# A softmax with relative-position bias: the last row of the fourth chunk's first load as two transfers, over 120 and over 8 partitions

## The chip, the cores and the metric

The kernel runs on one core of a Trainium2 chip. The metric is the device time of one execution in microseconds; where several runs are shown, their median counts. Of the core's engines the kernel uses the vector engine (DVE), the scalar engine (ACT), the synchronisation engine (SP), which only issues transfers, and for two tiny set-up instructions GpSimd (POOL). Transfers between the chip's memory (DRAM) and the on-chip memory (128 partitions) are carried by 16 DMA engines. SP and ACT each have a queue of their own on all 16.

## The reference

For two batches, eight heads and 2112 positions, `logits` holds 2 x 8 square matrices of 2112 x 2112 float32. To each element a bias is added that depends on its head and on the clipped distance of its row and column, and then a softmax goes along each row.

```
pos = np.arange(S)
rel = pos[:, None] - pos[None, :]
rel_clipped = np.clip(rel, -max_rel, max_rel) + max_rel      # max_rel = 16
bias = rel_bias[:, rel_clipped].copy()                        # (H, S, S)
logits = logits + bias[None, :, :, :]
logits = logits - logits.max(axis=-1, keepdims=True)
exp = np.exp(logits)
return (exp / exp.sum(axis=-1, keepdims=True)).astype(np.float32)
```

285 MB are read and 285 MB are written; the arithmetic per element is small.

## The kernel before, in words

**Tiling.** The 8 x 2112 rows of one batch are dealt to the 128 partitions in runs of RP = 132 neighbouring rows, so 16 partitions share a head. The kernel works through a partition's 132 rows in K = 11 rounds of G = 12 rows. A round has NBUF = 4 chunks: two of R = 6 rows of the first batch and the same two of the second. A chunk is thus 128 partitions x 6 rows x 2112 columns (on each partition 50,688 contiguous bytes in DRAM), and there are 44 chunks. Chunk m of every round lives in buffer X[m]; the four buffers are all there is. The order listings call the four buffers X_58 to X_61.

**Loads (SP).** Lines 97 and 98 issue the loads of the first round's four chunks at once, one after the other, without a wait. Then the loop of lines 99 to 102 goes over rounds and chunks: it waits until the store from X[m] has landed (semaphore st[m]) and issues the next load into X[m]. A load raises ld[m] by 16 when all of it has landed.

**The DVE's loop** (lines 222 to 226). At the start of a round `window` copies the bias row that this round needs (L172). For each chunk `add` waits for ld[m] and then goes through the six rows (L186): it adds the bias, negates, and takes the row's extremum into `nmax`. `scale` waits until the ACT has done the six exponentials, takes the reciprocals of the sums (L210) and multiplies four of the six rows (L213). Then comes the next chunk.

**The ACT's loop** (lines 227 to 231). `exps` takes each row as soon as the DVE has added to it and writes the exponentials and their sums (L197); `scale_rest` multiplies the last two rows (L218); `store` waits until all six rows are scaled and issues the chunk's store to `out` (L95).

**What sets the order.** Nothing but the code's order on each engine and the semaphores; there is no scheduler. L88 is the helper `take`, which waits for a semaphore and lowers it again. On every DMA engine the loads stand in SP's queue and the stores in ACT's, each in the order of issue.

**Around these** stand a set-up that builds the bias row on each partition from `rel_bias` (lines 119 to 169), for which the ACT issues one small load over 4 partitions (L122), and at the end SP's wait for the last four stores (lines 103 and 104).

The lines that the change touches are the four first loads (97, 98) and the wait at the head of `add` (183).

Of the kernel before, what the change touches and what calls it, by code (L numbers as in the profile page):

```python
# [15 lines left out]
def kernel(  # L16
# [6 lines left out]
    nc = tc.nc  # L23
    P = 128
    B, H, S, S2 = logits.shape
# [3 lines left out]
    RP = H * S // P  # L29
# [4 lines left out]
    NBUF = 4  # L34
    R = 6
    M = NBUF // B
    G = M * R
# [6 lines left out]
    X = [io.tile([P, R * S], FP32, tag=f"X{b}", name=f"X{b}") for b in range(NBUF)]  # L44
# [22 lines left out]
    def view(t, offset, dims):  # L67
        return bass.AP(tensor=t.tensor, offset=t.offset + offset, ap=[[list(t.ap[0])[0], P]] + dims)

    def rows(t, k, m):  # L70
        return bass.AP(
            tensor=t.tensor, offset=t.offset + (m // M) * (H * S * S) + (m % M) * R * S + k * (G * S), ap=[[RP * S, P], [1, R * S]],
        )

    with tc.tile_critical(no_gpsimd_drain=True):  # L75
        ld = [nc.alloc_semaphore(f"ld{b}") for b in range(NBUF)]
        st = [nc.alloc_semaphore(f"st{b}") for b in range(NBUF)]
# [2 lines left out]
        scaled = nc.alloc_semaphore("scaled")  # L80
        inv = nc.alloc_semaphore("inv")
        rb = nc.alloc_semaphore("rb")
        zero = nc.alloc_semaphore("zero")
        idx = nc.alloc_semaphore("idx")
        dve = nc.alloc_semaphore("dve")

        def take(eng, sem, n):
            eng.wait_ge(sem, n).then_inc(sem, -n)  # L88

        def load(k, m):  # L90
            nc.sync.dma_start(out=X[m][:, :], in_=rows(logits, k, m)).then_inc(ld[m], 16)

        def store(k, m):
            take(nc.scalar, scaled, R)
            nc.scalar.dma_start(out=rows(out, k, m), in_=X[m][:, :]).then_inc(st[m], 16)  # L95

        for m in range(NBUF):
            load(0, m)
        with nc.Fori(0, K - 1, 1, engines=[ENG.SP]) as k:
            for m in range(NBUF):  # L100
                take(nc.sync, st[m], 16)
                load(k + 1, m)
# [3 lines left out]
        v = nc.vector  # L106
# [6 lines left out]
        def settle():  # L113
# [9 lines left out]
            out=bass.AP(tensor=F2.tensor, offset=F2.offset, ap=[[Q * step, P // Q], [1, H * W]]),  # L123
            in_=bass.AP(tensor=rel_bias.tensor, offset=rel_bias.offset, ap=[[0, P // Q], [1, H * W]]),
# [15 lines left out]
        for o, n, s, op in ((eq, NB, q, ALU.is_equal), (lt, NB, q, ALU.is_lt), (hsel, H, h, ALU.is_equal),  # L140
# [24 lines left out]
                           in_=view(reg, 1, [[1, NB - 1], [0, RP - W]])))  # L165
# [9 lines left out]
        def row(m, i):  # L175
            return X[m][:, i * S : (i + 1) * S]

        def col(t, m, i, n=1):
            c = m * R + i
            return t[:, c : c + n]  # L180

        def add(m):
            take(v, ld[m], 16)
            for i in range(R):
                x = G - 1 - (m % M) * R - i
                v.tensor_tensor_reduce(  # L186
                    out=row(m, i), in0=row(m, i), in1=F2[:, x : x + S],
                    scale=-1.0, scalar=BIG, op0=ALU.add, op1=ALU.min, accum_out=col(nmax, m, i),
                ).then_inc(added, 1)
# [32 lines left out]
        with nc.Fori(0, K, 1, engines=[ENG.DVE]) as k:  # L222
            window(k)
            for m in range(NBUF):
                add(m)
                scale(m)
        with nc.Fori(0, K, 1, engines=[ENG.Activation]) as k:
            for m in range(NBUF):
                exps(m)
                scale_rest(m)  # L230
                store(k, m)
# [31 lines left out]
```

## Time and profile before

| | |
|---|---|
| three runs | 1325.74, 1325.94, 1336.57 us |
| median | 1325.94 us |
| the profiled execution, first to last instruction (span) | 1323.8 us |
| DVE busy | 866.2 us, 65% |
| ACT busy | 757.2 us, 57% |
| bytes moved by DMA | 570.98 MB, 431 GB/s over the span |
| each of 44 loads and 44 stores | 6336 KB |
| median from issue to landing | loads 38.4 us, stores 59.0 us |

The profile is of one execution. Its span leaves out what lies before the first instruction and after the last; it is 2.1 us, or 0.16%, below the median of the three runs. The busy times of the engines overlap each other. A landing is the moment when all 16 DMA engines have reported their share of a transfer. In the DMA views a queue's row holds its packets, the MB they carry, and the time they took as a share of 16 engines over the stretch; q1 is SP's queue, q10 ACT's. Timeline rows start with the start and the length in microseconds, then engine, line, operation and tiles; in square brackets is the idle time before the instruction, and what ended it.

### The profile page before, as it was taken

The numbers are of one execution on the slowest core, as the hardware profiler recorded it, in microseconds if no ns is written. First come the engines' busy times: TensorE is split into PE (matmuls) and PEld (weight loads), VectorE is DVE, ScalarE is ACT, GpSimd is POOL, SyncE is SP. The second block draws the span as 40 slices with busy tenths as digits, with TensorE's granted clock in tenths as the row PEclk, the third lists the DMA queues.
The fourth block names the chain that finished last, engine by engine and source line by source line (L and its number), as shares of the span: only waits on it lengthen the run. The fifth ranks groups of instructions, "written<-read, shape, count | busy, mean of one in ns | idle before, by whom it ended". The sixth has DMA issues, their size and how long they took to land. (4 is left out here: it accounts for less than half of the span.)

```text
span 1323.8 us, 2109 instructions
## 1 busy us (share of the span) xinstructions
DVE 866.2 (65%) x781; ACT 757.2 (57%) x627; POOL 0.4 (0%) x6
## 2 busy tenths in 40 slices
DVE  6886666566766675576667666556766576566662
ACT  3776655556666555555656555555666565555663
POOL 0000000000000000000000000000000000000000
DMA  9999999999999999999999999999999999999998
GB/s 417 417 423 435 441 435 423 441 438 421 440 441 427 430 441 435 424 440 438 424 437 440 437 423 440 440 421 438 441 432 426 441 437 423 440 440 423 437 441 369
DMA packets 12682, 570.98 MB, mean 431 GB/s; under 512 B 1412, under 2 KB 1416, under 8 KB 1416
## 3 DMA queue, kind: packets, MB, share of 16 engines
q1 hardware_dynamic: 6336, 285.48, 50.0%
q10 hardware_dynamic: 6344, 285.48, 49.8%
q14 instruction: 2, 0.02, 0.0%
HBM read 285.48 MB, written 285.47 MB: 431 GB/s over the span
## 5 line engine op out<-in xcount | busy, mean ns | idle before, releaser
L197 ACT ACTIVATE X<-X,nmax 128x2112 f32<-128x2112 f32 x264 | 542.6, 2055 | 505.1 <-DVE nmax L186 472.4
L186 DVE CUSTOM_DVE_ANT_0 X<-X,F 128x2112 f32<-128x2112 f32 x264 | 605.2, 2354 | 319.1 <-DVEq L88 319.1
L213 DVE TENSOR_SCALAR X<-X,rec 128x2112 f32<-128x2112 f32 x176 | 220.3, 1315 | 2.8
L218 ACT ACTIVATE X<-X,rec 128x2112 f32<-128x2112 f32 x88 | 176.1, 2048 | 17.2 <-DVE rec L210 12.2
L210 DVE RECIPROCAL rec<-tot 128x6 f32<-128x6 f32 x44 | 8.4, 191 | 106.2 <-DVEq L88 106.2
L197 ACT ACTIVATION_READ_ACCUMULATOR X<-X,nmax 128x1 f32 x264 | 49.2, 186 | 0.0
L197 ACT ACT_TABLE_LOAD x11 | 14.1, 1283 | 22.6 <-ACTq L88 19.9
L172 DVE COPY F<-F 128x2123 f32 x11 | 26.0, 2361 | 0.5 <-DVEq L88 0.5
L186 DVE DVE_READ_ACCUMULATOR2_ANT nmax<- 128x1 f32 x264 | 21.6, 82 | 0.0
L144 DVE LOAD_MASK_SELECT F<-F x1 | 0.0, 14 | 6.2 <-DMA F<-in_rel_bias_dram 6.2
L164 DVE COPY F<-own 128x1485 f32<-128x1485 f32 x1 | 1.7, 1698 | 0.0
L120 DVE MEMSET F<- 128x264 f32 x1 | 0.3, 278 | 1.1 <-SPq L75 1.1
L142 DVE TENSOR_SCALAR Z<-rec,Z 128x16 f32<-128x16 f32 (+2 forms) x5 | 0.8, 233 | 0.1
L163 DVE TENSOR_TENSOR F<-F,own 128x528 f32<-128x528 f32 x1 | 0.7, 717 | 0.1
L160 DVE TENSOR_TENSOR F<-Z,own 128x528 f32<-128x528 f32 x1 | 0.7, 705 | 0.0
L150 DVE TENSOR_REDUCE own<-F 128x33 f32<-128x264 f32 x1 | 0.6, 609 | 0.1
L147 DVE TENSOR_TENSOR F<-F,Z 128x264 f32<-128x264 f32 x1 | 0.4, 429 | 0.1
L144 DVE STREAM_SHUFFLE F<-F 128x264 f32<-128x264 f32 x1 | 0.4, 442 | 0.0
L158 DVE SCALAR_TENSOR_TENSOR own<-Z,own 128x16 f32<-128x16 f32 x1 | 0.2, 235 | 0.2 <-DVEq L88 0.2
L155 DVE TENSOR_SCALAR own<-Z,own 128x16 f32<-128x16 f32 x1 | 0.2, 235 | 0.2 <-DVEq L88 0.2
L166 DVE COPY F<-own 128x115 f32<-128x115 f32 x1 | 0.3, 271 | 0.0
L168 DVE COPY F<-own 128x115 f32<-128x115 f32 x1 | 0.3, 271 | 0.0
(11 smaller groups left out, 1.6 us busy)
## 6 DMA issues: line engine op xcount, KB each, us to landing
X<-in_logits_dram SPq DMA_DIRECT2D x44, 6336.0 KB, 38.4
out_dram<-X ACTq DMA_DIRECT2D x44, 6336.0 KB, 59.0
F<-in_rel_bias_dram ACTq DMA_DIRECT2D x1, 4.1 KB
```

The source lines that it names most:

```text
L142: then(v.tensor_scalar(out=o, in0=num[:, 0:n], scalar1=s, scalar2=None, op0=op))
L144: then(v.stream_shuffle(out=T, in_=T, mask=[0] * Q))
L150: then(v.tensor_reduce(out=rbK, in_=view(F2, H * W, [[1, W], [W, H]]), axis=mybir.AxisListType.X, op=ALU.add))
L160: then(v.tensor_tensor(out=bands, in0=view(eq, 0, [[1, NB], [0, W]]), in1=view(rbK, W - 1, [[0, NB], [-1, W]]), op=ALU.mult))
L163: then(v.tensor_tensor(out=bands, in0=bands, in1=view(rest, 0, [[1, NB], [0, W]]), op=ALU.add))
L164: then(v.tensor_copy(out=view(F, C0 + W, [[RP, NB - 1], [1, RP - W]]), in_=view(reg, 1, [[1, NB - 1], [0, RP - W]])))
L172: then(v.tensor_copy(out=F2[:, 0:SW], in_=F[:, bass.ds(RP - G - k * G, SW)]))
L186: v.tensor_tensor_reduce(out=row(m, i), in0=row(m, i), in1=F2[:, x : x + S], scale=-1.0, scalar=BIG, op0=ALU.add, op1=ALU.min, accum_out=c ...
L197: nc.scalar.activation(out=row(m, i), in_=row(m, i), func=ACTF.Exp, scale=-1.0, bias=col(nmax, m, i), accum_out=col(tot, m, i),).then_inc( ...
L210: v.reciprocal(out=col(rec, m, 0, R), in_=col(tot, m, 0, R)).then_inc(inv, 1 if m < NBUF - 1 else NBUF + 1)
L213: v.tensor_scalar_mul(out=row(m, i), in0=row(m, i), scalar1=col(rec, m, i)).then_inc(scaled, 1)
L218: nc.scalar.activation(out=row(m, i), in_=row(m, i), func=ACTF.Copy, scale=col(rec, m, i),).then_inc(scaled, 1)
```

## The change

The first load of the fourth chunk (m = 3, buffer X_61) is issued in three pieces: rows 0 to 4 of all 128 partitions, which still raise ld[3]; then row 5 of partitions 0 to 119; then row 5 of partitions 120 to 127. The last two raise a new semaphore, head3. The DVE's `add` waits, for this buffer, also until head3 is at least 32. That wait doesn't lower head3, so from the second round on it is met at once. All later loads, and the first loads of the other three chunks, are as before.

```
@@ part: a view of DRAM that takes rows a to b of n partitions from p on
+    def part(t, k, m, a, b, p=0, n=P):
+        return bass.AP(
+            tensor=t.tensor, offset=t.offset + (m // M) * (H * S * S) + ((m % M) * R + a) * S + k * (G * S) + p * RP * S,
+            ap=[[RP * S, n], [1, (b - a) * S]],
+        )
+
...
+        head3 = nc.alloc_semaphore("head3")
...
+        def load_part(eng, m, a, b, sem, p=0, n=P):
+            eng.dma_start(out=X[m][p : p + n, a * S : b * S], in_=part(logits, 0, m, a, b, p, n)).then_inc(sem, 16)
+
...
-        for m in range(NBUF):
+        for m in range(NBUF - 1):
             load(0, m)
+        UP = P - P // 16
+        load_part(nc.sync, NBUF - 1, 0, R - 1, ld[NBUF - 1])
+        load_part(nc.sync, NBUF - 1, R - 1, R, head3, 0, UP)
+        load_part(nc.sync, NBUF - 1, R - 1, R, head3, UP, P - UP)
...
         def add(m):
             take(v, ld[m], 16)
+            if m == NBUF - 1:
+                v.wait_ge(head3, 32)
             for i in range(R):
```

SP's instructions at the start of the program, before the change: the four first loads, and then the first rows of the loop (ISA is the wait for a store).

```order
L91 DMA X_58<-in_logits_dram 128x12672
L91 DMA X_59<-in_logits_dram 128x12672
L91 DMA X_60<-in_logits_dram 128x12672
L91 DMA X_61<-in_logits_dram 128x12672
L99 UNCONDITIONAL_BRANCH
L91 ISA
L91 DMA X_58<-in_logits_dram 128x12672
```

The same place of SP with the change (the numbers of the lines are those of the changed kernel):

```order
L98 DMA X_58<-in_logits_dram 128x12672
L98 DMA X_59<-in_logits_dram 128x12672
L98 DMA X_60<-in_logits_dram 128x12672
L101 DMA X_61<-in_logits_dram 128x10560
L101 DMA X_61<-in_logits_dram 120x2112
L101 DMA X_61<-in_logits_dram 8x2112
L113 UNCONDITIONAL_BRANCH
L98 ISA
L98 DMA X_58<-in_logits_dram 128x12672
```

One transfer of 12672 columns has become three, of 10560, 2112 and 2112 columns, in the same place ahead of the loop. On the DVE and the ACT no instruction is added or moved; only the first add of buffer X_61 waits for two semaphores in place of one.

## The prediction

> **What bounds the kernel now.** I read the page first: the busy shares, the DMA line and the queues.
>
> ```profile
> DVE 866.2 (65%) x781; ACT 757.2 (57%) x627; POOL 0.4 (0%) x6
> ...
> DMA  9999999999999999999999999999999999999998
> ...
> DMA packets 12682, 570.98 MB, mean 431 GB/s; under 512 B 1412, under 2 KB 1416, under 8 KB 1416
> ...
> q1 hardware_dynamic: 6336, 285.48, 50.0%
> q10 hardware_dynamic: 6344, 285.48, 49.8%
> ```
>
> No compute engine is above 65%, and the DMA engines are busy in every slice. q1 carries the loads (SP), q10 the stores (ACT). 6336 packets for 44 loads are 144 each: 128 data packets, one per partition (six rows, 50,688 B), and 16 small ones that raise the semaphore, one per DMA engine. So an engine gets 8 data packets and one count per transfer.
>
> Next the DMA view of one whole round of four chunks in the middle, 200 to 319.6 us:
>
> ```profile
> q1 hardware_dynamic: 576, 25.95, 50.1%
> q10 hardware_dynamic: 575, 25.90, 50.0%
> ```
>
> 51.85 MB over 16 engines and 50,688 B are 63.9 packets per engine in 119.6 us: **1.871 us per packet**. The whole kernel has 704 per engine, 1317 us of the 1323.8 us span, so at most 6 or 7 us can be gained anywhere. The waits agree: the DVE's largest wait is that of its add (L186) for a load, through the semaphore instruction of L88.
>
> ```profile
> DVE X L186 <- DVEq L88: 319.1, 42, 8.5
> ```
>
> What is left to decide is how the two queues stand to each other. I call **lead** the number of data packets by which an engine's load queue is ahead of its store queue. The DMA view from 0 to 85.3 us (about where the fourth load has landed), then from 85.3 to 115.1 us:
>
> ```profile
> q1 hardware_dynamic: 588, 26.56, 74.1%
> q10 hardware_dynamic: 204, 9.13, 24.7%
> ...
> q1 hardware_dynamic: 144, 6.49, 50.3%
> q10 hardware_dynamic: 144, 6.49, 50.3%
> ```
>
> One packet on all 16 engines is 0.811 MB, so at 85.3 us the lead is (26.56 - 9.13) / 0.811 = 21.5, and 44.0 packets have gone. After that the queues take strict turns, 144 to 144, and the lead stays. It matters once, at the end. The timeline there, the DMA view from 1281.4 to 1324 us, and the windows (columns: stretch, length, the engines' busy times, clock, DMA share, GB/s):
>
> ```profile
> 1281.59 2.36 DVE L186 CUSTOM_DVE_ANT_0 X<-X,F 128x2112 f32<-128x2112 f32 x1 [8.54 <-DVEq L88]
> ...
> 1303.34 0.34 ACTq L95 DMA_DIRECT2D out_dram<-X  x1
> ...
> q10 hardware_dynamic: 369, 16.27, 88.2%
> ...
> 1305.00:1320.00 15.00, 0.00 (x0) 0.00 (x0) 0.00 (x0) 1.00 0.91 395
> 1320.00:1322.00 2.00, 0.00 (x0) 0.00 (x0) 0.00 (x0) 1.00 0.06 25
> ```
>
> When the last load lands, 16.27 / 0.811 = 20.1 store packets per engine are left. Eight belong to the last store, 12.1 stand before it: 22.6 us of transfers, to 1304.0 us. The last chunk's compute takes 21.75 us, to the issue at 1303.34. It is a tie: the last store enters the queue just as the queue runs dry. **Every packet of lead that is lost costs 1.87 us there.** The last row has a share of 0.06, one engine of sixteen: one straggler finishes about a packet after the others.
>
> Two more views, the sources L91 and L95, give issue to landing (min/median/max), first of loads, then of stores:
>
> ```profile
> L91 SPq DMA_DIRECT2D X<-in_logits_dram x44: 332/333/549, 1.0 to 1244.2; - x44
> ...
> DMA to landing us min/median/max: 17.6/38.4/82.8
> ...
> DMA to landing us min/median/max: 19.3/59.0/60.5
> ```
>
> 17.6 us is a load with the engines to itself: 15.0 for 8 packets, 2.6 around them. The shortest store, the last one, takes 1.7 us more: the straggler.
>
> **The change part by part.**
>
> *Issue.* Six DMA issues on SP in place of four: two more at 0.333 us. The four end before 3 us, and the fourth load's first packet comes after 24 others, past 45 us. Hidden; without that cover 0.67 us.
>
> *The added wait.* head3 is waited for by the DVE's first add of the fourth chunk in all 11 rounds, beside ld3. A semaphore instruction on the DVE's queue takes 21 ns:
>
> ```profile
> L88 DVEq EVENT_SEMAPHORE  x118: 21/21/21, 1.6 to 1298.0; - x118
> ```
>
> Behind it stand the chunk's six adds, and behind these the ACT's exps. Ten of the eleven times the count was reached long before: 0.2 us in all, most of it in the DVE's waits for loads, 0.02 us at the end. The eleventh is the fourth chunk of the first round, which now waits for three landings.
>
> *Where the bytes go.* The small load of rel_bias shows what a transfer over few partitions does: q10 has 8 packets more than q1, and these are its 4 partitions and 4 counts, one engine per partition. By that I estimate that the 8-partition transfer puts one 8,448 B row on each of 8 engines, and the 120-partition transfer 8 rows on each of 15; the sixteenth engine has none. The Trainium skill, "DMA: Bandwidth & Descriptors", section "Why a DMA increments its semaphore by 16 and not by 1", says the same: the largest count up to 16 that divides the partitions, lowest engines first; the trace agrees for the 4. So eight engines carry 1/6 packet more (0.3 us), and one 1.33 packets less (2.5 us).
>
> *Turns.* This is the main term. The start, in the timeline and then the DMA view from 0 to 44.7 us (q1) and from 44.7 to 85.3 us:
>
> ```profile
> 40.38 0.38 ACTq L95 DMA_DIRECT2D out_dram<-X  x1
> ...
> 61.69 0.34 ACTq L95 DMA_DIRECT2D out_dram<-X  x1
> ...
> 83.35 0.34 ACTq L95 DMA_DIRECT2D out_dram<-X  x1
> 85.36 2.36 DVE L186 CUSTOM_DVE_ANT_0 X<-X,F 128x2112 f32<-128x2112 f32 x1 [2.58 <-DVEq L88]
> ...
> 106.81 2.36 DVE L172 COPY F<-F 128x2123 f32 x1
> 107.14 0.34 ACTq L95 DMA_DIRECT2D out_dram<-X  x1
> ...
> q1 hardware_dynamic: 396, 18.45, 99.3%
> ...
> q10 hardware_dynamic: 196, 9.12, 51.9%
> q1 hardware_dynamic: 192, 8.11, 46.4%
> ```
>
> By 44.7 us the load queue has moved 18.45 / 0.811 = 22.75 packets; then the first store begins, and the queues take turns. Before: 1.25 packets of load 2 with its count, then 8 and a count: 11.25 turns, 9.25 packets of bytes, against 11.25 store turns, 10.25 of them data. 19.5 packets are 36.5 us, so 81.2; the DVE in fact starts at 85.36, 4.2 us later (start of the first store, turns not in step), and I add the same 4.2 afterwards.
>
> After, on the eight engines with all three transfers: 1.25 + 1, then 8 + 1 of five rows, 8 + 1 of one row, 1 + 1: **22.25 turns** for 9.42 packets of bytes. If a turn is a packet whatever its size, 22.25 store turns pass beside them, 20.25 of data. The first three stores, issued at 40.38, 61.69 and 83.35, hold 24, so there are enough. 29.7 packets are 55.5 us: 100.2, with the 4.2 **104.4 us**, 19.0 later than now.
>
> The DVE is free (the copy of L172 follows the fourth chunk), so chunk 3 and its store move by 19.0: issue at 126.1, first packet some 1.3 us later, half of the 2.6: 127.4. By then the stores have run out at 24 packets, and the loads go on alone (the fifth was issued when the first store landed). In all 44.0 + (127.4 - 85.3) / 1.871 = 66.5 packets have gone, 42.5 of them loads: lead 18.5, **3.0 less**.
>
> No byte is lost there: in the middle both queues stay filled, so the trace will look alike. At the end the last load lands 3.0 x 1.871 = 5.6 us later, the last store is issued at 1308.9, and the engines stand idle before it. That also absorbs the straggler: 17.6 us, not 19.3, from issue to landing. End 1326.5 in place of 1303.34 + 19.3 = 1322.6: **+3.9 us**. The span of 1323.8 is 2.1 below the median of 1325.94; carried to the median, 1329.8.
>
> *Bounds of this term.* Below: a turn goes by bytes, the lead stays, 0. Above: the store queue's own need. A chunk's store is issued 21.75 us after the landing and starts 1.3 later; 23.05 us of turns are 6.2 store packets, with its own 8 a lead of 14.2 in the measure that is 20.1 now. Below that the store queue runs dry each chunk and the loads catch up, so the lead cannot stay lower: 5.9 packets, 11.0 us, less 1.7: +9.3. I take +3.9, since the strict 144 to 144 is nearest to turns by packet. That row alone cannot show turns between unequal packets, as all are equal.
>
> **The rivals.**
>
> *Turns by bytes.* Then the lead stays, and what counts is the straggler. If it is the engine that is relieved, -1.7 + 0.3: 1324.5, the only way to be faster; if another, +0.3: 1326.2. For it: the 0.06 row shows just one engine late, by less than the 2.5 us taken off one engine. Against: the profile does not name the straggler. In the same page's "Latency and other measured facts" the Trainium skill calls engines 7 and 15 usually slower, for transfers that GpSimd issues; no run here shows it.
>
> *Turns in blocks.* If an engine's nine packets of a transfer went as one turn, load 3 would be three blocks against the 24 store packets there are; the fourth store would start near 134 us, where 44.0 + 26.0 packets less 24 leave 46 loads, a lead of 22: it is kept, and the time is about 1326. The Trainium skill, in the section "Queues, rings and completion order" of that page, has such a rule: an engine drains some 9 to 17 descriptors of a queue before it turns to the next. Against it speaks the DMA view from 60 to 62 us, where engines that began together serve both queues:
>
> ```profile
> q10 hardware_dynamic: 10, 0.51, 58.5%
> q1 hardware_dynamic: 8, 0.41, 46.8%
> ```
>
> *The lead falls to its floor.* If the loads cannot catch up by 3.9 packets while the stores are out (because the next load waits for a store that lands late on one engine), the end is +9.3: 1335.2.
>
> *Over 1% slower: engines out of step.* SP issues a load only when the old store has landed on all 16 engines. The relieved engine keeps its lead near 21.5, so its stores land latest, and the others, at 18.5, wait for it with their next load. An engine's load queue holds 24 packets beyond the landed store, less 1.4 for the 2.6 us of a new issue; it runs dry if the mean of the two leads is over 22.6. It is 20.0 here, so the price is nothing; past the point, 0.2 packets in each of 40 later loads would cost 15 us: 1341.
>
> **How the numbers follow.** Forecast (lead down by some 3): 0.52, 1327.5 to 1332. Lead kept and straggler relieved: 0.20 (1324.5); lead kept, by bytes or by blocks, nothing relieved: 0.10 (1326). Floor: 0.12 (1335.2). Out of step: 0.06 (1341). The range takes in all but the last and some scatter: 1323.8 to 1336.5. One per cent, 13 us, is about what a measurement of this kernel can tell from no change: the three runs before span 1325.74 to 1336.57. Slower by over 1%: the last case and a little of the floor, 0.08. Faster by over 1% the 1317 us of packets exclude nearly: 0.01.
>
> **What would show it.** The first add of chunk 3 near 104 us in place of 85.36, the store behind it near 126; a stretch before it with q1 packets alone; in the middle round again 576 and 575; at the end an idle stretch of some 5 us before the last store, no 0.06 row, 17.6 us from its issue to landing. If chunk 3 still starts by 90 us, turns are not by packet and the time lies near 1325. If the middle has DMA shares well under 1, the engines are out of step and I am wrong by more.

## The result, and the profile after

| | before | changed |
|---|---|---|
| median of 6 runs each | 1325.97 us | 1335.3 us |
| lowest to highest | 1325.72 to 1336.57 | 1332.13 to 1336.16 |
| span of the profiled execution | 1323.8 us | 1333.2 us |

The ratio is 1.0057, with a 95% interval of 1.0034 to 1.008: the change costs half a per cent. (That ratio isn't the one of the two medians, which is 1.0070.) It lies within the 1% that the prediction took for no change, and within its range, but at +9.3 us it is more than twice the forecast +3.9. Two of the six runs before, at 1332.1 and 1336.57 us, are as long as those of the changed kernel. The two profiled spans differ by the same 9.4 us, so the profile can be used to find the difference.

First the page of the changed kernel: the DMA line, the packets and the two queues (q1 loads, q10 stores; packets, MB, share of 16 engines).

```profile
DMA  9999999999999999999999999999999999999996
...
DMA packets 12833, 570.98 MB, mean 428 GB/s; under 512 B 1435, under 2 KB 1439, under 8 KB 1439
...
q1 hardware_dynamic: 6487, 285.48, 49.7%
q10 hardware_dynamic: 6344, 285.48, 49.5%
```

q1 has 151 packets more than the 6336 of before. These are 128 row packets for the last row and 23 counts, 15 + 8: the transfer over 120 partitions used 15 engines, that over 8 used 8. The Trainium skill's rule on this ("DMA: Bandwidth & Descriptors", section "Why a DMA increments its semaphore by 16 and not by 1": the largest number up to 16 that divides the partitions) agrees with the 23. The DMA line differs from that of before in its last digit alone, 6 in place of 8: there is less work at the very end.

The start of the changed kernel: two timeline rows (the first add of the fourth chunk, then that chunk's store), and the DMA view from 44.7 to 85.3 us and from 115 to 127 us.

```profile
104.84 2.36 DVE L202 CUSTOM_DVE_ANT_0 X<-X,F 128x2112 f32<-128x2112 f32 x1 [22.03 <-DMA X<-in_logits_dram]
...
126.62 0.34 ACTq L105 DMA_DIRECT2D out_dram<-X  x1
...
q10 hardware_dynamic: 223, 10.49, 59.7%
q1 hardware_dynamic: 207, 6.65, 38.3%
...
q1 hardware_dynamic: 113, 4.97, 95.6%
q10 hardware_dynamic: 24, 0.46, 8.8%
```

The chunk starts at 104.84 (forecast 104.4) and its store is issued at 126.62 (126.1). In between the two queues exchange almost equal numbers of packets, 223 to 207, but very unequal bytes, 10.49 to 6.65 MB. Then the loads go on nearly alone, since the stores have run out.

What that does to the lead can be read from the DMA view from 0 to 160 us, first of the changed kernel and then of the kernel before:

```profile
q1 hardware_dynamic: 1070, 41.72, 61.5%
q10 hardware_dynamic: 584, 26.06, 37.8%
```

```profile
q1 hardware_dynamic: 940, 42.78, 62.9%
q10 hardware_dynamic: 556, 25.35, 36.6%
```

By the difference of the MB over 0.811 the lead is 19.3 packets, and was 21.5. One such reading swings by about one packet with the moment at which it is cut. The mean over six cuts, at 150, 155, ... 175 us, is 18.8 and was 21.7: **2.9 packets less, where 3.0 were forecast.** The issue groups of the page point the same way without any cut (KB each, median us from issue to landing), again changed kernel first:

```profile
out_dram<-X ACTq DMA_DIRECT2D x44, 6336.0 KB, 50.7
X<-in_logits_dram SPq DMA_DIRECT2D x43, 6336.0 KB, 47.0
```

```profile
X<-in_logits_dram SPq DMA_DIRECT2D x44, 6336.0 KB, 38.4
out_dram<-X ACTq DMA_DIRECT2D x44, 6336.0 KB, 59.0
```

A store lands 8.3 us earlier and a load 8.6 us later. In strict turns one packet of position is worth two packet times, 3.74 us, so both are 2.2 to 2.3 packets, somewhat less than 2.9. (A landing waits for the last of the 16 engines, the lead is their mean.)

The middle round of the changed kernel, 200 to 319.6 us:

```profile
q1 hardware_dynamic: 575, 25.90, 50.5%
q10 hardware_dynamic: 570, 25.65, 49.5%
```

51.55 MB in place of 51.85. The forecast said that it would look alike; 0.37 packets per engine are missing, 0.7 us in this round.

The end of the changed kernel: the last chunk's first add and its store, the DMA view from 1289 and then from 1293.7 to 1333 us, the windows (stretch, length, busy times of DVE, ACT and POOL, clock, DMA share, GB/s), and the landing of stores (min/median/max).

```profile
1293.94 2.36 DVE L202 CUSTOM_DVE_ANT_0 X<-X,F 128x2112 f32<-128x2112 f32 x1 [8.62 <-DVEq L95]
...
1315.68 0.34 ACTq L105 DMA_DIRECT2D out_dram<-X  x1
...
q10 hardware_dynamic: 322, 13.89, 73.1%
q1 hardware_dynamic: 2, 0.05, 0.3%
...
q10 hardware_dynamic: 269, 11.96, 70.5%
...
1300.00:1305.00 5.00, 5.00 (x5) 4.74 (x5) 0.00 (x0) 1.00 1.03 446
1305.00:1310.00 5.00, 2.70 (x4) 4.62 (x6) 0.00 (x0) 1.00 0.21 91
1310.00:1315.00 5.00, 4.74 (x5) 4.00 (x2) 0.00 (x0) 1.00 0.02 10
1315.00:1320.00 5.00, 0.46 (x1) 0.00 (x0) 0.00 (x0) 1.00 0.76 324
...
DMA to landing us min/median/max: 16.4/50.7/52.5
```

The idle stretch before the last store is there, about 10 us long (shares 0.21 and 0.02) where some 5 were forecast. Now the sum. The last load landed at 1281.59 before and at 1293.94 now, 12.35 us later:

- At 1289.0 only 2 load packets are left, one of data (0.05 MB) and one count: a single engine has not finished. The stores left are 13.89 / 0.811 = 17.1 per engine, against 20.1 when the last load landed before. Those 3.0 packets are 5.6 us, as forecast; the other 1.8 us of the 7.4 up to here are pace lost on the way. The trace's records of single packets show most of it: between 130 and 1280 us the 50,688 B packets of the changed kernel took 1.4 us per engine longer in all than those before, 1.2 us of it between 200 and 500 us.
- From 1289.0 to 1293.94 the DVE waits 4.9 us for that one engine's last load packet and its count. The records have the packet at 1289.52, 1.87 us long, and the count at 1293.26: a store packet's turn lies between them.
- The last store takes 16.4 us from issue to landing, not 19.3: -2.9.

12.35 - 2.9 = 9.45, and the spans differ by 9.4.

### The profile page after: what moved, and what is told of

It reads as the page before. It is cut to its first block, busy times and chain, and to the rows that moved or that the text cites. A ratio compares the mean times of both kernels' runs of the same rounds, so it can differ in the third digit from the quotient of the medians.

```text
span 1333.2 us, 2111 instructions
## 1 busy us (share of the span) xinstructions
DVE 866.2 (65%) x781; ACT 757.2 (57%) x627; POOL 0.4 (0%) x6
## 5 line engine op out<-in xcount | busy, mean ns | idle before, releaser
L202 DVE DVE_READ_ACCUMULATOR2_ANT nmax<- 128x1 f32 x264 | 21.7, 82 | 0.0
```

Source lines behind the costliest of these rows:

```text
L202: v.tensor_tensor_reduce(out=row(m, i), in0=row(m, i), in1=F2[:, x : x + S], scale=-1.0, scalar=BIG, op0=ALU.add, op1=ALU.min, accum_out=c ...
```

## The experiments

The questions were these. Is it the additional turns of the load queue, or the uneven dealing over engines, or the small packets? Why more than 3.9? And, after the first results, how far does it go?

For comparison, each kernel's lead is the mean over the six cuts at 150 to 175 us, as above. Each ratio is to the kernel before in the same job (medians of 1325.96 to 1326.92 us). A lead is that of the one profiled execution, a median that of all runs; e10's and e11's profiled executions, of 1336.17 and 1535.64 us, are no typical ones.

| kernel | lead | median us | ratio (95% interval) |
|---|---|---|---|
| e6_store_only | 22.0 | 1334.19 | 1.0028 (1.0002 to 1.0054) |
| before | 21.7 | 1326 | 1 |
| e9_late_store0 | 21.5 | 1326.05 | 0.9975 (0.995 to 1.0001) |
| e5_store_too | 21.3 | 1327.52 | 1.0015 (0.9994 to 1.0035) |
| e5b_store_128 | 21.3 | 1327.2 | 0.9996 (0.9972 to 1.002) |
| e4_six_rows | 20.5 | 1347.57 | 1.0159 (1.0138 to 1.0179) |
| e1_second_chunk | 19.8 | 1332.86 | 1.0053 (1.0034 to 1.0072) |
| changed kernel | 18.8 | 1335.3 | 1.0057 (1.0034 to 1.008) |
| e10_64_64 | 17.6 | 1343.03 | 1.0095 (1.0055 to 1.0135) |
| e3_halves | 17.3 | 1506.95 | 1.1353 (1.1321 to 1.1385) |
| e2_row_128 | 17.0 | 1504.74 | 1.1331 (1.1264 to 1.1397) |
| e8_late_store3 | 16.4 | 1532.26 | 1.1524 (1.1469 to 1.1579) |
| e12_half | 16.4 | 1538.85 | 1.1561 (1.1507 to 1.1615) |
| e11_no_scale | 16.4 | 1494.21 | 1.1238 (1.116 to 1.1315) |

### e1_second_chunk: the same split in the second chunk

```
-        for m in range(NBUF - 1):
-            load(0, m)
+        load(0, 0)
+        (the second chunk, m = 1: rows 0-4 over 128, row 5 over 120, row 5 over 8)
+        for m in range(2, NBUF):
+            load(0, m)
...
-            if m == NBUF - 1:
+            if m == 1:
                 v.wait_ge(head3, 32)
```

> The same three transfers and the same added wait, but in the second chunk's first load, which has landed (33 us) before the first store moves a packet (44 us). Theory of turns: the small packets alternate with nothing, the lead stays at 21.5, the fourth chunk still starts at 85 to 86 us, and the time is that of the kernel before, 1325.5 to 1327.5 us. Rival, the imbalance: the engine that carries no last row runs ahead of the others and the loads that wait for all 16 engines pay for it; that engine is relieved here just as much, so the time stays near 1333 to 1336 us.

It took 1332.86 us, not 1325.5 to 1327.5, and so lies next to the 1333 of the rival. Two stretches of windows of e1, while the small packets pass (same columns as above), and then of the kernel before:

```profile
30.00:34.00 4.00, 2.50 (x4) 3.64 (x5) 0.00 (x0) 1.00 1.01 230
34.00:38.00 4.00, 3.04 (x4) 3.63 (x4) 0.00 (x0) 1.00 1.10 306
```

```profile
30.00:34.00 4.00, 2.48 (x4) 3.64 (x5) 0.00 (x0) 1.00 0.94 406
34.00:38.00 4.00, 3.06 (x4) 3.63 (x4) 0.00 (x0) 1.00 0.94 406
```

With no stores beside them the one-row packets move 230 GB/s, and 306 where the next full ones come in, in place of 406. In the records such a packet takes 0.60 us on average here, and 0.33 us in the changed kernel, where it has stores beside it. So this was no clean test: it lost bytes of its own, (406 - 230) x 4 us and (406 - 306) x 4 us, together 1.1 MB or 1.4 packets per engine, 2.5 us, and its lead fell by 1.9 packets (3.6 us). As in the changed kernel, the last chunk waits for late engines, here two: from 1290 us on only one data packet of the last load still begins (0.05 MB), another is under way, and the chunk starts at 1294.45, 4.5 us later. The last store lands 2.9 us sooner. These are 7.7 of the 9.9 us by which its profiled span, 1333.7 us, is longer; the rest was not found. So e1 does not exclude the rival; e5 and e10 below speak against it.

### e2_row_128 and e3_halves: whole transfers over 128 partitions

e2 is the changed kernel with the last row in one transfer; e3 splits the load into three rows and three rows.

```
-        load_part(nc.sync, NBUF - 1, R - 1, R, head3, 0, UP)
-        load_part(nc.sync, NBUF - 1, R - 1, R, head3, UP, P - UP)
+        load_part(nc.sync, NBUF - 1, R - 1, R, head3)          # e2; e3: rows 0 to 2 and rows 3 to 5
...
-                v.wait_ge(head3, 32)
+                v.wait_ge(head3, 16)
```

> The fourth chunk's last row goes as one transfer over all 128 partitions, so that no engine is relieved, and every engine has 18 turns for this load in place of 9. Theory of turns: 20.25 turns of loads after 44.7 us are 17.3 us, the 18.25 store packets beside them 34.1 us, with the 4.2 us of excess the fourth chunk starts at 100 us, its store at 123 us, lead 16.3 or 5.2 less, and the time is 1326 + 9.7 - 1.7 = 1334 us. Rival, the imbalance: without a relieved engine the time falls back to 1326 to 1328 us.

> The fourth chunk's first load goes as three rows and three rows, each over 128 partitions: 18 turns an engine as with five rows and one, but packets of 25,344 bytes and none that is small. Theory of turns: only the number of turns counts, so the fourth chunk starts again near 100 us and the time is 1333 to 1336 us. Rival, small packets cost by themselves (a gap around each, or a bad row size): no packet is small here, and the time is 1326 to 1328 us.

The start came as turns by packet have it, and in the end both fell far outside what any theory had. The first add of the fourth chunk in e3 (in e2 it is at 100.56), and then the page's GB/s line of e2, 40 slices of 37.4 us:

```profile
100.92 2.36 DVE L200 CUSTOM_DVE_ANT_0 X<-X,F 128x2112 f32<-128x2112 f32 x1 [17.89 <-DMA X<-in_logits_dram]
```

```profile
GB/s 412 425 422 427 420 414 418 420 389 372 386 371 390 387 355 390 387 387 389 370 387 371 390 387 355 390 385 379 383 387 387 371 389 390 356 390 390 391 255 190
```

The chunk starts at the same time whether the two transfers are of five rows and one or of three and three: what delays it is their number, not their size. But after eight slices, about 300 us, the pace breaks from 420 to some 384 GB/s and never recovers. The DMA view of e2 from 600 to 720 us:

```profile
q10 hardware_dynamic: 526, 23.42, 48.5%
q1 hardware_dynamic: 500, 22.71, 46.4%
```

In the kernel before the same stretch has:

```profile
q1 hardware_dynamic: 583, 26.31, 50.6%
q10 hardware_dynamic: 578, 26.05, 50.2%
```

46.13 MB in place of 52.36, 12% less. The shares make 94.9% in place of 100.8, so about half of the loss is engines without a packet; for the other half the packets take longer, 2.00 us in the mean of the full-size records here against 1.87. With **two full transfers, dealt evenly**, the kernel is 13% slower, while the uneven split of the changed kernel costs 0.6%.

### e4_six_rows: all six rows over 120 and over 8 partitions

```
-        load_part(nc.sync, NBUF - 1, 0, R - 1, ld[NBUF - 1])
-        load_part(nc.sync, NBUF - 1, R - 1, R, head3, 0, UP)
-        load_part(nc.sync, NBUF - 1, R - 1, R, head3, UP, P - UP)
+        load_part(nc.sync, NBUF - 1, 0, R, ld[NBUF - 1], 0, UP)
+        load_part(nc.sync, NBUF - 1, 0, R, head3, UP, P - UP)
```

> All six rows go over 120 and over 8 partitions, two transfers: fifteen engines keep 9 turns for this load, eight of them have 2 more (one data packet and one count), and the sixteenth carries nothing of it, so the imbalance is six times as large (15 us ahead in place of 2.5). Theory of turns: the fourth chunk starts some 5.6 us later, at 91 us, the lead falls by about 2, and the time is 1328 to 1332 us. Rival, the imbalance: six times the imbalance costs more than the changed kernel's 9 us, and the time is above 1338 us.

The fourth chunk started at 106.04, not 91, and the time is 1347.57. Its windows, while those transfers run:

```profile
60.00:85.00 25.00, 20.52 (x19) 17.53 (x15) 0.00 (x0) 1.00 0.96 300
85.00:115.00 30.00, 8.96 (x7) 6.29 (x6) 0.00 (x0) 1.00 0.97 343
```

The kernel before moves 450 and 433 GB/s there. The loss is (450 - 300) x 25 us + (433 - 343) x 30 us = 6.5 MB, 8.0 packets per engine, 15 us of the 21.6. The time is that of the rival (above 1338), but whether it is the uneven dealing that costs is not shown: e12 below has such a hole with even dealing. What the two share is full-size rows over part of the partitions, and these cost at once and in bytes. That is another loss than that of the changed kernel, whose rate has no such hole. Why packets stood so long there (the DMA share remains 0.96) the rows do not tell.

### e5_store_too and e5b_store_128: give the store queue as many turns

e5 keeps the changed kernel's three loads and splits the very first store in the same way; e5b does so with e2's two loads and two stores. The first round of the SP's and the ACT's loops is written out for it.

```
         def store(k, m):
             take(nc.scalar, scaled, R)
+            if isinstance(k, int) and m == 0:       # e5; e5b: rows 0-4 and row 5, both over 128
+                for a, b, p, n in ((0, R - 1, 0, P), (R - 1, R, 0, UP), (R - 1, R, UP, P - UP)):
+                    nc.scalar.dma_start(out=part(out, k, m, a, b, p, n), in_=X[m][p : p + n, a * S : b * S]).then_inc(st[m], 16)
+                return
```

> The changed kernel, and the first store of all is split in the same way: five rows over 128 partitions, the last row over 120 and over 8. The store queue then has as many additional turns as the load queue, 11 on eight engines, 9 on seven. Theory of turns: the small store packets meet the small load packets, the fourth chunk starts within a few us of 85, the store queue never runs dry, the lead stays near 21.5, and the time falls to 1325 to 1329 us. Rival: what costs is that the engines no longer move together after a transfer that is not dealt evenly (the last load lands 5 us later on one engine than on the rest): the time stays at 1332 to 1336 us.

> The kernel with the last row over all 128 partitions (1505 us), and its first store is split likewise, five rows and one row. Theory: the 170 us come from the moment at which the store queue has run dry and all 16 engines take up stores at once (14 of 16 then read together and write together, and packets that took 1.87 us take 2.0 to 2.6). Here the store queue does not run dry, so the engines keep the pattern of the kernel before, and the time is 1325 to 1335 us. Rival: the single-row packets over all partitions do the harm by themselves; then the time stays above 1450 us.

The DMA view of e5 from 44.7 to 85.3 us, and three timeline rows of it:

```profile
q10 hardware_dynamic: 346, 9.07, 52.9%
q1 hardware_dynamic: 331, 7.76, 45.3%
...
86.68 2.36 DVE L209 CUSTOM_DVE_ANT_0 X<-X,F 128x2112 f32<-128x2112 f32 x1 [3.97 <-DMA X<-in_logits_dram]
...
1283.59 2.36 DVE L209 CUSTOM_DVE_ANT_0 X<-X,F 128x2112 f32<-128x2112 f32 x1 [8.53 <-DVEq L95]
...
1305.36 0.34 ACTq L109 DMA_DIRECT2D out_dram<-X  x1
```

All of the changed kernel's load transfers are there, with their small packets, their uneven dealing and their wait. Now the stores use up as many turns, the fourth chunk starts at 86.68 again, the last store is issued at 1305.36 (before: 1303.34), and the median is 1327.52. e5b does the same to e2: 1327.2 in place of 1504.74, and its fourth chunk starts at the time of before again:

```profile
85.29 2.36 DVE L207 CUSTOM_DVE_ANT_0 X<-X,F 128x2112 f32<-128x2112 f32 x1 [2.59 <-DMA X<-in_logits_dram]
```

This is the decisive pair: **the cost lies in the turns that one queue has and the other has not.** What is left for uneven dealing and small packets themselves is the +1.2 us of e5 over the kernel before in its job, within its interval.

### e8_late_store3 and e9_late_store0: a delay that was none

After e2 the question was why a packet or two more of lead lost should break the pace. One idea was the moment at which the fourth store comes in: into an empty store queue, with all engines in step, that is, all loading or all storing at one time. e8 is e2 with about 1 us of useless work on the ACT ahead of that store; e9 puts the same work ahead of the very first store of the kernel before, as a measure of what the edit does by itself. Both have the ACT's first round written out ahead of its loop.

```
         def store(k, m):
             take(nc.scalar, scaled, R)
+            if isinstance(k, int) and m == 3:        # e9: m == 0
+                nc.scalar.activation(out=Z[:, 0:1024], in_=own[:, 0:1].to_broadcast([P, 1024]), func=ACTF.Copy, scale=1.0)
```

> The kernel with the last row over all 128 partitions (1505 us), and the ACT does one useless instruction of about 1 us, half a packet, just before it issues the fourth chunk's first store. If it is the engines' step at the moment when stores are taken up again that makes the 1505 us, another moment gives another pattern of engines that read and write together, and the time moves by tens of us, most likely down, to 1340 to 1450 us. If the lost lead alone made it, the time moves by 1 us or so and stays near 1505 us.

> The kernel before, with one useless instruction of about 1 us on the ACT just before the very first store. No transfer is split. Theory of turns alone: the loads get half a packet ahead, the lead grows by 0.5, the time stays at 1325.5 to 1327 us. Rival, the step of the engines matters by itself: which engines read and which write together is settled when the first store is taken up; another pattern gives some other time, 1328 to 1340 us, without any change in turns or bytes.

Neither store was delayed. The timeline of e8 there, and a stretch of its windows:

```profile
121.66 1.03 ACT L106 ACTIVATE Z<-own 128x1024 f32<-128x1024 f32 x1 [1.16 <-ACTq L95]
121.67 0.34 ACTq L107 DMA_DIRECT2D out_dram<-X  x1
...
130.00:160.00 30.00, 17.86 (x17) 16.89 (x14) 0.00 (x0) 1.00 0.98 367
```

The transfer is issued 10 ns after the useless work has begun, not after its 1.03 us: the issue does not wait for the work ahead of it. In e9 it is the same (40.38 and 40.40, where the kernel before has 40.38). e9, at 1326.05, thus shows only that the written-out round costs nothing. In e8, with that round written out, the store came 0.7 us earlier than in e2 (122.34). So e8 is e2 with a slightly earlier fourth store: the lead is 16.4 in place of 17.0, the pace is down to 367 GB/s at once and not after 300 us, and the time is 1532.26. The idea of the moment was not tested by it. But the packet records speak against engines in step as the cause: from 200 to 300 us of e8, with the pace broken, the numbers of engines that load and that store differ by 3.4 on average, while in e6 below they differ by 14.5 of 16 and its pace holds (435 to 438 GB/s).

### e12_half and e10_64_64: fewer turns, or even dealing

e12 gives each engine about 15 turns for the fourth load, e10 deals the changed kernel's last row over 64 and 64 partitions.

```
+        load_part(nc.sync, NBUF - 1, 0, R, ld[NBUF - 1], 0, P // 2)              # e12
+        load_part(nc.sync, NBUF - 1, 0, R - 1, head3, P // 2, P // 2)
+        load_part(nc.sync, NBUF - 1, R - 1, R, head3, P // 2, P // 2)
...
+        load_part(nc.sync, NBUF - 1, R - 1, R, head3, 0, P // 2)                 # e10, after rows 0-4 over 128
+        load_part(nc.sync, NBUF - 1, R - 1, R, head3, P // 2, P // 2)
```

> The fourth chunk's first load goes as six rows over partitions 0 to 63, five rows over 64 to 127, and the last row over 64 to 127: every engine gets the same, 12 data packets and 3 counts, 15 turns in place of 9 (18 in the kernel with the row over 128). Theory of turns: 17.25 load turns after 44.7 us with 15.3 store packets beside them, the fourth chunk starts at 95 us, its store's first packet comes at 118 us, and by then 21.5 of the 24 store packets have gone: the store queue does not run dry. So the lead falls by 3.0, as I forecast for the changed kernel, and with the store queue never dry the engines are not set in step: 1330 us, between 1328 and 1336. Rival: a lead under 19 breaks the pace by itself, with or without a dry queue; then it is above 1400 us.

> As the changed kernel, but the last row over 64 and 64 partitions in place of 120 and 8: 19 turns on every engine, nobody relieved. Theory: the store queue runs dry as in the changed kernel (fourth chunk near 102 us, its store near 124), and what spares the changed kernel the breakdown is that 120 and 8 are dealt unevenly, so that the engines don't take up the stores in step. Here all are dealt alike, and the time is 1470 to 1540 us. Rival: three transfers, or later stores, are what spares it: 1330 to 1340 us.

The fourth chunk's first add, e12 and then e10:

```profile
106.94 2.36 DVE L201 CUSTOM_DVE_ANT_0 X<-X,F 128x2112 f32<-128x2112 f32 x1 [24.16 <-DMA X<-in_logits_dram]
```

```profile
102.11 2.36 DVE L201 CUSTOM_DVE_ANT_0 X<-X,F 128x2112 f32<-128x2112 f32 x1 [19.35 <-DMA X<-in_logits_dram]
```

e10 started where turns by packet put it, at 102. It deals evenly over 16 engines and is yet slower than the changed kernel: 1343.03, at a lead of 17.6; two of its seven runs, the profiled one among them, are at 1334 to 1336. So the relief of one engine is not needed for the loss. e12 missed: 106.94 in place of 95, with 308 GB/s from 60 to 85 us, a hole like that of e4 (both send full-size rows over part of the partitions). It therefore says nothing on the number of turns. But its lead of 16.4 went with a broken pace once more, though its fourth store came at 128.71, later than in the changed kernel: that speaks against the moment of that store as the cause.

### e6_store_only: the turns on the other side

The kernel before with the first store as rows 0 to 4 and row 5, each over 128 partitions, should raise the lead.

```
-        load_part(...)   (the three pieces of the fourth load)
+        load(0, NBUF - 1)
...
+            if isinstance(k, int) and m == 0:
+                for a, b, p, n in ((0, R - 1, 0, P), (R - 1, R, 0, P)):
+                    nc.scalar.dma_start(out=part(out, k, m, a, b, p, n), in_=X[m][p : p + n, a * S : b * S]).then_inc(st[m], 16)
+                return
```

> The kernel before, with only its very first store split, five rows and one row over 128 partitions. Theory of turns: 9 more store turns put the loads ahead, the lead goes from 21.5 towards its upper end near 22.6, the tie at the end becomes a small reserve, and the time stays at 1325 to 1327 us; runs above 1330 us, of which the kernel before has some, become rarer if they come from a lost tie. Rival: a split over all partitions sets the engines in step whichever queue it is in: above 1400 us.

The lead rose only to 22.0, and the fourth chunk started at 82.57, 2.8 us earlier than before. The times fall into two groups: 4 of 12 runs lie at 1325.28 to 1328.94, 8 at 1332.96 to 1337.12. The profiled execution is one of the second group (1334.88), so it can show what a long run looks like. The DMA view of e6 from 0 to 800 and from 0 to 1200 us:

```profile
q1 hardware_dynamic: 4015, 181.62, 52.7%
q10 hardware_dynamic: 3783, 163.78, 47.3%
...
q1 hardware_dynamic: 5919, 266.77, 51.6%
q10 hardware_dynamic: 5730, 251.93, 48.5%
```

The lead is 22.0 at 800 us and 18.3 at 1200 us, where the kernel before (268.19 and 250.86 MB) has 21.4 and the changed kernel (266.72 and 251.72 MB) 18.5. This execution lost its lead on the way, late, and then ended like the changed kernel: its last store was issued at 1312.67. A larger lead at the start is therefore no safeguard. The landing records of the stores from X[0] show one engine falling behind. It lands 0.1 us after the fifteenth at 195.8 us, 2.2 at 676.4, 4.9 at 918.4 and 9.0 at 1160.9. SP issues the next load only when this engine too has landed, so the other engines' loads come later and later. The kernel before has such runs as well (7 of the 25 in the job of e5 lie between 1329.85 and 1336.34); whether they are the same slip was not seen, since no long run of it was profiled.

### e11_no_scale: more time in hand for the stores

The last idea for the broken pace was that a store isn't ready when its turn comes. e11 is e2 without the scalings of all chunks and without the reciprocals of three of four; it leaves out the division by the row sums, so that a store can be issued some 5 us earlier.

```
-                scale(m)
+            take(v, expd, R)
+            v.reciprocal(out=col(rec, NBUF - 1, 0, R), in_=col(tot, NBUF - 1, 0, R)).then_inc(scaled, R)
...
-                scale_rest(m)
```

> The kernel with the last row over all 128 partitions (1505 us), but without the division by the row sums: the reciprocals of three chunks in four and all scalings are left out, and the output is not the softmax. A chunk then takes some 16 to 17 us from landing to store in place of 21.75, and needs a lead of 12.7 in place of 14.2, while I expect the lead after the start to settle near 16, as in the kernels that broke down (16.1 to 16.9). Theory of the reserve: what breaks the pace is that the stores come too late for the queue; with 5 us more in hand the pace holds, and the time is 1320 to 1345 us. Rival: a lead of 16 to 17 packets, two chunks, is bad by itself (loads and stores of an engine then go to the same place of two chunks at once): the pace breaks as before, above 1400 us. If the lead settles elsewhere, the run only adds a point.

1494.21 us, 12.4% slower: the pace broke with the additional time in hand as well, and the rival of the expectation, above 1400 us, came out. Its profile is of an execution of 1535.64 us, longer than its other four, and only its start is used here: the lead of 16.4. The idea fell. The packet records show where the time goes: in e8 and e12 between 600 and 720 us 15.8 and 15.6 of the 16 engines have a full-size packet under way on average, so they hardly lack work, but such a packet takes 2.18 and 2.12 us. In the kernel before and the changed one it takes 1.87.

## Why the prediction was right, and where it was not

**Issue, the added wait, the bytes on the engines.** These were costed at 0.2 us, and e5, which has all of them, is 1.2 us above before. (The three issues took 0.29 to 0.53 us, not 0.333, but they begin before 4 us and stay hidden.) The estimate of 15 and 8 engines is confirmed by the 151 packets.

**Turns.** Right in kind and size. Start 104.84 (104.4), store 126.62 (126.1), lead down by 2.9 (3.0), loads alone before the store, and e2, e3 and e10 at 100.56, 100.92 and 102.11 where the same working gives 100, 100 and 102. The undoing in e5 and e5b shows that this is the cause. The rival "turns by bytes" falls with 10.49 against 6.65 MB, and "turns in blocks" with the store at 126.62 in place of 134 and a lead that was not kept. The Trainium skill's rule of 9 to 17 descriptors per turn ("DMA: Bandwidth & Descriptors", section "Queues, rings and completion order") isn't what these queues did here, if a row packet of the profile is one of its descriptors.

**"No byte is lost there: in the middle both queues stay filled."** Put at nothing, it was 1.8 us: 0.37 packets per engine are missing in the middle round alone.

**"At the end the last load lands 3.0 x 1.871 = 5.6 us later."** This is the term that failed. It landed 12.35 us later. 5.6 is right for all engines but one. The forecast treated the 16 engines as one with a mean lead, and thought of the straggler only at the last store, where it was said to be absorbed. But the DVE waits for all 16 engines of each load, so a straggler there costs its whole delay: 4.9 us. In the kernel before, the loads had no such straggler. Its DMA view from 1279.5 to 1282 us has of q1 only counts:

```profile
q10 hardware_dynamic: 16, 0.81, 74.9%
q1 hardware_dynamic: 5, 0.00, 0.1%
```

In the trace's single landing records of the changed kernel's last load, one engine is first at 1280.8, fourteen follow from 1287.1 to 1288.65, and one comes at 1293.8. The first is ahead of the fourteen by more than 6 us, some 3.4 packets, near the 2.9 that the engines lost on average. I take it to be the relieved engine, though the records do not name it: in e10, where none is relieved, the first engine of the last load lands 0.4 us before the middle one, here 6.8. If so, the relief brought that engine nothing but an earlier end, and the straggler is another.

The straggler wasn't made at the start. In the landings of buffer X[0]'s loads the last engine is 0.01 us after the fifteenth at 125.4 us, 0.9 at 601.6, 1.6 at 841.5 and 4.6 at 1203.4. It doesn't come from uneven dealing either: e10's last load ends with one engine 3.2 us after the fifteenth. In the kernel before an engine falls behind too, but there it shows in the stores (X[0]: 0.06 us after the fifteenth at 75.6, 1.8 at 1273.9), and not in the last load. Why an engine falls behind stays open.

**"17.6 us, not 19.3, from issue to landing."** It was 16.4. The forecast took the shortest load for it, the only transfer of before that had the engines to itself; the last store is 1.2 us shorter.

**The rival "floor", +9.3.** Its time, 1335.2, is the measured one, but not for its reason. All engines' lead would have had to fall to 14.2; at 1289, when fifteen engines have their last load, the stores left are 17.1. When the sixteenth has it, at 1293.7, they are 11.96 / 0.811 = 14.7, but only because the others went on storing meanwhile. So the agreement is luck, and so is it that the range, which reached up to this case, held the time. And its second use was wrong: the text held that the lead cannot stay below that floor, "so" +9.3 bounds the term above. Five kernels with 16.4 to 17.3 at the start are 168 to 212 us slower. The bound assumed that the pace holds at any lead. The range held the time, but the edge beyond it was not foreseen: e2, 1.8 packets lower in lead than the changed kernel, is 169 us slower than it.

**The rival "engines out of step", 1341.** Half of it is there: from the second round on one engine's stores land well after all others (X[0]: 193.86 against 190.76 us, later 555.27 against 550.97). Whose they are the records do not say, and that the others' loads ran dry for it no row shows: the shares of the middle round make 100%. Engines out of step did matter, by one straggler's last load.

**What stays open.** Lead at the start orders the kernels, except e4 with its own loss and e6 with its late slip: 21.3 to 21.7 within 0.3%, 17.6 to 19.8 at +0.5 to +1%, 17.3 and below broken. That is an association over 14 kernels, and 17.3 and 17.6 lie closer together than one reading swings. For the break, stores that are not ready in time are excluded as its cause as far as e11 reaches, and engines in step, taken alone, by e6; the moment of the fourth store has e12 against it, but the kernel that should have moved it did not. What is seen is that full-size packets take 2.0 to 2.2 us instead of 1.87. The rival in e11's expectation, that a lead of two chunks (16 packets) is bad in itself, fits the starts of all five broken kernels, but no run isolates it.

## What to carry to other kernels

Where two queues share the DMA engines, they here took turns by packet whatever its size, so a transfer that is split hands bandwidth to the other queue; count turns, not bytes, and give both queues the same count if the balance matters (e5, e5b). When an engine of compute waits for a transfer on all 16 DMA engines, reckon with the last of them and not with their mean. And a forecast that the pace will hold needs its own evidence: here the time rose by at most 1% as the lead fell to 17.6 packets (e4, which lost bytes of its own, apart), and by 12 to 16% at 17.3 and below.

## What the runs showed of the hardware that was not expected

- With loads and stores of equal size in strict turns the 16 engines carry 433 GB/s at a lead of 18.8 packets and, in e2, 384 GB/s (46.13 MB from 600 to 720 us) after a start at 17.0: 2.11 us per packet and engine in place of 1.87. In e8 and e12 the packets alone are longer, 2.18 and 2.12 us with 15.8 and 15.6 engines at work; in e2 they take 2.00 us, and engines also stand idle.
- Packets of one row, 8,448 B, alone on the engines moved 230 GB/s, full ones of 50,688 B 406 GB/s (e1). Beside stores their cost was turns, not rate: 0.33 us each in place of 0.60.
- Transfers of full-size rows over part of the partitions left the engines at 300 to 343 GB/s for 55 us (e4) and at 308 for 25 us (e12), though the DMA share stayed at 0.96 or more.
- A transfer's issue on the ACT's queue went out 10 to 20 ns after a 1.03 us activation ahead of it had begun, so that work put there delayed nothing (e8, e9).
- An execution can lose 3 to 4 packets of lead between 800 and 1200 us while one engine's stores fall behind by 9 us (e6, 22.0 to 18.3), and then takes as long as the changed kernel.
